# Odd layer's scan: the 128x128 transposes of each level become 64x64 products with the identity, and two products by tokens share one PSUM tile

## The chip, the cores and the metric

The kernel runs on one core of a Trainium2 chip. The metric is the device time of one execution in microseconds, the median of three runs.

## What is computed

The reference is a stack of two blocks of two layers each, on 512 tokens (and 256 context tokens) of width 1024. The change touches one part of the first block's odd layer: a recurrent scan with eight heads of 64 channels, run in two directions, first over the context and then over the tokens.

```python
def wkv7_scan(state0, p, d, reverse, emit):
    ...
    def step(S, inp):
        w_t, k_t, v_t, kk_t, a_t = inp[:5]
        sa = jnp.einsum('bhvk,bhk->bhv', S, kk_t)
        S = (S * w_t[:, :, None, :] - sa[..., None] * (kk_t * a_t)[:, :, None, :]
             + v_t[..., None] * k_t[:, :, None, :])
        return S, (jnp.einsum('bhvk,bhk->bhv', S, inp[5]) if emit else None)
```

The kernel computes this scan in chunks of 64 tokens. Within a chunk the 64 dependent steps become a triangular 64x64 system for each head, whose inverse X is built up in levels: blocks of 2, 4, ..., 32 rows are joined to blocks of twice the size.

## The kernel before, in words

The function `rwkv` holds the scan. Its work comes in **units**, `unit(d, i)`: one direction `d` (two) and one chunk `i` (twelve), 24 units in all, and in **blocks**, `block(d, g)`: the inputs of two chunks of one direction, 12 in all. Every unit and block is a generator; a loop over ticks starts a unit every third tick and a block nine ticks ahead of its first unit, and moves all that are alive by one step in each tick, so that six units or so are under way at once. What comes out of this is then ordered once more, for each engine, by the scheduler of the language, which weighs it by costs of its own; so a change in one step can move other instructions by a few places.

The eight heads lie as four groups of two: 64 partitions hold one head, the other 64 another. `prod` (line 1398) makes eight products of 64x64 tiles, one for each head. `pair` takes one of three PSUM tiles of two banks (pool `rwps`); the products of a head on the upper and on the lower partitions go to different banks. `seen` is the view by which a product is read back. In the profile these tiles are called `rw`.

One unit makes, in order: A (copied by ScalarE, line 1498) and X's first form (VectorE, lines 1502 and 1503); B (line 1509) and, for chunks of tokens, rb (line 1514), each with a PSUM tile of its own; a transposed copy kt of two inputs (lines 1521 and 1523); bv (line 1528); and then five levels. A level is

```python
for e in range(2):
    nc.tensor.transpose(ps[:, 0, P * e:P * e + P], X[:, 2 * e:2 * e + 2]..., ident)   # 1536
prod(ps, "J", "N", (grp(A), (lambda g: blk(X[:, g]))), base=256, step=32, n=32)
nc.scalar.copy(two(xt), ...)                                                          # 1539
nc.vector.tensor_tensor(out=two(w), ...)                                              # 1541
yield
prod(ps, "N", "J", (grp(xt), grp(w)), step=32, n=32)
nc.vector.tensor_tensor(out=xb, in0=xb, in1=s, op=ALU.subtract)                       # 1549
```

The transposes are two instructions on whole 128x128 tiles, all other products of the unit are on 64x64 tiles. After the levels come bv's correction, un (line 1561), the new state N (lines 1571 and 1572) and the output (lines 1583 to 1586, into the tile that the profile calls x).

A block makes, in this order: the low-rank products `ru` and `ra` (line 1447, TensorE, four instructions of 128x128 each), their tanh `th` (1448, ScalarE), `ld` (1458, GpSimd), the running sum `L` (1461, VectorE), `av` (1459) and `b` (1464) on GpSimd, exponentials on ScalarE (1468 to 1473), and on VectorE `kd`, `E` and the second `b` (1475 to 1481).

Of the kernel before, what the change touches and what calls it, by code (L numbers as in the profile page):

```python
# [12 lines left out]
ALU = mybir.AluOpType  # L13
# [3 lines left out]
P = 128  # L17
# [4 lines left out]
T = TX + TC  # L22
# [254 lines left out]
class Prog:  # L277
# [31 lines left out]
    c = v  # L309
# [1054 lines left out]
    def rwkv(self, R, mod, inner, parts, more):  # L1364
# [5 lines left out]
        nc, a = self.nc, self.a  # L1370
        DEC = float(np.exp(-0.5))
        with ExitStack() as es:
# [7 lines left out]
            i64 = self.c("i64")  # L1380
# [3 lines left out]
            pair = lambda: pps.tile([P, 1024], F32, tag="rw", name="rw").rearrange("p (b c) -> p b c", b=2)  # L1384
            of_c = lambda t_: t_.rearrange("p g c t -> p g (c t)")

            def prod(ps, lam, mu, *terms, base=0, step=64, at=0, n=64):

                lb, mb = LAY[lam][0], LAY[mu][0]
                bits = [0, 0, 0]  # L1390
                for bits[3 - lb - mb] in range(2):
                    for i, (L, Rb) in enumerate(terms):
                        for bits[lb] in range(2):
                            for bits[mb] in range(2):
                                g = 2 * bits[LAY[lam][1]] + bits[LAY[lam][2]]
                                h = HALF[bits[lb]]
                                o0 = base + step * bits[3 - lb - mb] + at
                                nc.tensor.matmul(ps[HALF[bits[mb]], bits[lb], o0:o0 + n], L(g)[h], Rb(g)[h],  # L1398
                                                 start=i == 0, stop=i == len(terms) - 1)

            def seen(ps, lam, mu, base=0, step=64, at=0, n=64):

                v = ps[:, :, base:base + 2 * step].rearrange("p b (s w) -> p b s w", s=2)[:, :, :, at:at + n]
                return v if LAY[mu][1] == LAY[lam][0] else v.rearrange("p b s w -> p s b w")

            grp = lambda t_: (lambda g: t_[:, g])
            two = lambda t_: t_.rearrange("p (x y) w -> p x y w", x=2)
            mask = lambda d, i, n=1: (mk[:, d, i:i + n].rearrange("p m q -> p (m q)").unsqueeze(1).unsqueeze(1)
                                      .to_broadcast([P, 2, 2, 64 * n]))
            ident = self.c("ident")  # L1410
# [73 lines left out]
            def unit(d, i):  # L1484
                ci = chunk(d, i)
                isx = ci >= 4
                E, b_, kd_, gc_, vt = blocks[d, ci // 2]
                c = ci % 2
                e0, e1 = (lambda g: E[:, g, c, 0]), (lambda g: E[:, g, c, 1])
                b, kd, v = (lambda g: b_[:, g, c]), (lambda g: kd_[:, g, c]), (lambda g: vt[:, c, g])  # L1490
                gc = gc_[:, :, c]
                nn = P if isx else 64
                ev = lambda g: E[:, g, c].rearrange("p e t -> p (e t)")[:, :nn]

                ps = pair()
                prod(ps, "N", "J", (e0, b))
                A = sm("A", 5)
                nc.scalar.copy(two(A), seen(ps, "N", "J"))
                ps = pair()
                prod(ps, "N", "J", (b, e0))  # L1500
                X = sm("X", 6)
                nc.vector.tensor_tensor(out=two(X), in0=seen(ps, "N", "J"), in1=mask(1 - d, 0), op=ALU.mult)
                nc.vector.tensor_tensor(out=X, in0=i64s, in1=X, op=ALU.subtract)
                yield

                ps = pair()
                prod(ps, "N", "T", (kd, ev), step=P, n=nn)
                B = sm("B", 6, nn)
                nc.vector.tensor_tensor(out=two(B), in0=seen(ps, "N", "T", step=P, n=nn), in1=mask(d, 6, nn // 64), op=ALU.mult)
                if isx:  # L1510
                    ps = pair()
                    prod(ps, "N", "T", (b, e1))
                    rb = sm("rb", 6)
                    nc.vector.tensor_tensor(out=two(rb), in0=seen(ps, "N", "T"), in1=mask(d, 7), op=ALU.mult)
                yield
                if i < 11:

                    ps = pair()
                    for q, t_ in enumerate((kd_, b_)):
                        for j in range(2):  # L1520
                            nc.tensor.transpose(ps[:, q, P * j:P * j + P], t_[:, 2 * j:2 * j + 2, c].rearrange("p e t -> p (e t)"), ident)
                    kt = up.tile([P, 2, 4, 64], F32, tag="kt", name="kt", bufs=5)
                    nc.scalar.copy(kt.rearrange("p q g f -> p q (g f)"), ps[:, :, 0:256])
                yield
                ps = pair()
                prod(ps, "T", "J", ((lambda g: B[:, g, 0:64]), v))
                bv = sm("bv", 5)
                nc.scalar.activation(out=two(bv), in_=seen(ps, "T", "J"), func=AF.Copy, scale=-1.0)
                yield

                for l in range(1, 6):

                    blk = lambda t_: t_.rearrange("p (n two b) -> p n two b", two=2, b=1 << l)[:, :, 1 - d]
                    ps = pair()
                    for e in range(2):
                        nc.tensor.transpose(ps[:, 0, P * e:P * e + P], X[:, 2 * e:2 * e + 2].rearrange("p h c -> p (h c)"), ident)  # L1536
                    prod(ps, "J", "N", (grp(A), (lambda g: blk(X[:, g]))), base=256, step=32, n=32)
                    xt, w = sm("xt", 3), sm("w", 3, 32)
                    nc.scalar.copy(two(xt), ps[:, 0, 0:256].rearrange("p (e j r) -> p j e r", e=2, j=2))
                    m = mk[:, d, l, 0:32].unsqueeze(1).unsqueeze(1).to_broadcast([P, 2, 2, 32])  # L1540
                    nc.vector.tensor_tensor(out=two(w), in0=seen(ps, "J", "N", base=256, step=32, n=32), in1=m, op=ALU.mult)
                    yield
                    ps = pair()
                    prod(ps, "N", "J", (grp(xt), grp(w)), step=32, n=32)
                    xb = X.rearrange("p (x y) (n two b) -> p x y n two b", x=2, two=2, b=1 << l)[:, :, :, :, 1 - d]
                    s = seen(ps, "N", "J", step=32, n=32).rearrange("p x y (n b) -> p x y n b", b=1 << l)
                    if l == 5:
                        xb, s = xb[:, :, :, 0], s[:, :, :, 0]
                    nc.vector.tensor_tensor(out=xb, in0=xb, in1=s, op=ALU.subtract)
                    yield  # L1550

                N = state[d]
                if N is not None:
                    ps = pair()
                    prod(ps, "N", "J", (e0, grp(N)))
                    nc.vector.tensor_tensor(out=two(bv), in0=two(bv), in1=seen(ps, "N", "J"), op=ALU.subtract)
                yield
                ps = pair()
                prod(ps, "J", "T", (grp(X), grp(bv)))
                un = sm("un", 3)  # L1560
                nc.scalar.copy(two(un), seen(ps, "J", "T"))
                yield
                if i < 11:
                    ps = pair()
                    prod(ps, "T", "N", ((lambda g: kt[:, 0, g]), v), ((lambda g: kt[:, 1, g]), grp(un)))
                    N2 = sm("N", 3)
                    gcb = gc.unsqueeze(2).to_broadcast([P, 4, 64])
                    if N is None:
                        nc.vector.tensor_tensor(out=two(N2), in0=seen(ps, "T", "N"), in1=two(gcb), op=ALU.mult)
                    else:  # L1570
                        nc.vector.tensor_tensor(out=two(N2), in0=two(N), in1=seen(ps, "T", "N"), op=ALU.add)
                        nc.vector.tensor_tensor(out=N2, in0=N2, in1=gcb, op=ALU.mult)
                    state[d] = N2
                yield
                if isx:

                    ps = pair()
                    prod(ps, "N", "J", (grp(N), e1))
                    prod(ps, "T", "J", (v, (lambda g: B[:, g, 64:P])), (grp(un), grp(rb)), base=P)
                    c4 = ci - 4  # L1580
                    yy = two(y[:, :, 64 * c4:64 * c4 + 64])
                    if (c4 < 4) == (d == 0):
                        nc.scalar.copy(yy, seen(ps, "N", "J"))
                    else:
                        nc.vector.tensor_tensor(out=yy, in0=yy, in1=seen(ps, "N", "J"), op=ALU.add)
                    nc.vector.tensor_tensor(out=yy, in0=yy, in1=seen(ps, "T", "J", base=P), op=ALU.add)
                done.add((d, i))
# [485 lines left out]
    def ssd_part(self, n, hi, lo, sp, R):  # L2073
# [22 lines left out]
        def prep(g, r):  # L2096
            def feature(nm, j):
                def done(ps):
                    r[nm] = tl(nm, [n], 1 if nm == "B" else 2)
                    self.ssd_conv(j, ps, n, sp, cbuf, r[nm])  # L2100
                    yield
                    if nm == "B":
                        for _ in range(6):
# [365 lines left out]
```

## Time and profile before

| what | value |
|---|---|
| runs | 4059.23, 4055.31, 4044.3 us; median 4055.31 us |
| profiled execution | 4060.4 us, of it the span 4058.7 us |
| mean granted TensorE clock of the span | 0.968 |
| busy in the span | TensorE 94%, weight loads 77%, VectorE 58%, ScalarE 38%, GpSimd 7% |
| the scan | from 1390 to 1710 us of the span |

In the rows further down, PE is TensorE, PEld its weight loads (which overlap PE), DVE VectorE, ACT ScalarE, POOL GpSimd. `rw<-X,A 64*64 64x32 f32` is a product into tile rw of the operands X and A on a 64x64 tile of the array. An f32 product shows as two instructions, so a `prod` of eight products reads x16; a transpose shows as one. Busy times of TensorE overlap and their ends are modelled, so what a group costs is read from its start to the next group's start.

### The profile page before, as it was taken

The numbers are of one execution on the slowest core, as the hardware profiler recorded it, in microseconds if no ns is written. First come the engines' busy times: TensorE is split into PE (matmuls) and PEld (weight loads), VectorE is DVE, ScalarE is ACT, GpSimd is POOL, SyncE is SP. The second block draws the span as 40 slices with busy tenths as digits, with TensorE's granted clock in tenths as the row PEclk, the third lists the DMA queues.
The fourth block names the chain that finished last, engine by engine and source line by source line (L and its number), as shares of the span: only waits on it lengthen the run. The fifth ranks groups of instructions, "written<-read, shape, count | busy, mean of one in ns | idle before, by whom it ended". The sixth has DMA issues, their size and how long they took to land.

```text
span 4058.7 us, 68289 instructions
## 1 busy us (share of the span) xinstructions
PE 3832.5 (94%) x28564; PEld 3110.9 (77%) x28564; DVE 2348.8 (58%) x4086; ACT 1554.3 (38%) x2862; POOL 294.7 (7%) x310
## 2 busy tenths in 40 slices
PE   7999999999999898899999999999998999989998
PEld 5667788888877676678877877888887777767887
DVE  6556555545645455577664466455458788784334
ACT  4456321212445344342233333212126576663222
POOL 0222000000010011000000000000001222120000
PEclk8999999999999979999999998999998999999999
DMA  4221133333214311145541102333333233322232
GB/s 176 85 84 41 63 110 116 115 107 100 75 50 140 117 42 40 31 147 177 165 146 60 65 30 72 116 116 116 102 96 122 82 108 109 120 73 83 94 95 87
DMA packets 144196, 393.08 MB, mean 97 GB/s; under 512 B 14096, under 2 KB 45712, under 8 KB 142992
## 3 DMA queue, kind: packets, MB, share of 16 engines
q1 hardware_dynamic: 143888, 388.72, 29.0%
q8 instruction: 224, 3.67, 0.4%
q14 instruction: 84, 0.69, 0.1%
HBM read 374.38 MB, written 14.29 MB: 96 GB/s over the span
## 4 chain that ended last, share of the span: by engine, by line
PE 80%; DVE 9%; issue 4%; ACT 4%; DMA 1%; POOL 1%; SPq 0%; DVEq 0%; ACTq 0%; POOLq 0%
PE mm L418 18%; PE mm L359 15%; PE mm L361 15%; PE mm L363 15%; PE mm L388 4%; PE rw L1398 2%; PE y L900 2%; PE tp L887 2%; PE y L2342 1%; PE rw L1536 1%; DVE cva L2068 1%; DVE wlo L340 1%; PE s L817 1%; ACT whi L339 1%; PE s L818 0%
## 5 line engine op out<-in xcount | busy, mean ns | idle before, releaser
L339 ACT CAST whi<-w 128x1024 fp32r<-128x1024 f32 (+2 forms) x429 | 439.1, 1025 | 1588.0 <-PE mm L361 1004.3
L340 DVE TENSOR_TENSOR wlo<-w,whi 128x1024 fp32r<-128x1024 f32 (+2 forms) x429 | 518.0, 1208 | 329.9 <-ACT whi L339 321.2
L359 PE MATMUL mm<-fhi,whi 128*128 128x512 f32 x2016 | 610.0, 356 | 0.0
L361 PE MATMUL mm<-flo,whi 128*128 128x512 f32 x2016 | 609.4, 356 | 0.0
L363 PE MATMUL mm<-fhi,wlo 128*128 128x512 f32 x2016 | 607.5, 355 | 0.0
L363 PEld LDWEIGHTS mm<-fhi,wlo 128*128 128x128 f32 x2016 | 331.3, 187 | 61.3
L359 PEld LDWEIGHTS mm<-fhi,whi 128*128 128x128 f32 x2016 | 331.4, 187 | 60.8
L361 PEld LDWEIGHTS mm<-flo,whi 128*128 128x128 f32 x2016 | 331.4, 187 | 59.4
L475 DVE SCALAR_TENSOR_TENSOR wdot<-wmod,cb 128x1024 f32<-128x1024 f32 x288 | 352.0, 1222 | 9.6 <-ACT cb L469 3.6
L626 DVE SCALAR_TENSOR_TENSOR x<-mm,mod,x 128x512 f32<-128x512 f32 (+1 forms) x214 | 131.9, 643 | 339.4 <-PE mm L363 270.2
L738 DVE TENSOR_TENSOR g<-g,mm 128x512 f32<-128x512 f32 (+1 forms) x134 | 75.6, 590 | 403.4 <-PE mm L363 395.7
L359 PE MATMUL mm<-ah,whi 128*128 128x512 f32 x972 | 294.0, 356 | 0.0
L361 PE MATMUL mm<-al,whi 128*128 128x512 f32 x972 | 293.8, 356 | 0.0
L363 PE MATMUL mm<-ah,wlo 128*128 128x512 f32 x972 | 293.0, 355 | 0.7 <-DVE wlo L340 0.7
L363 PEld LDWEIGHTS mm<-ah,wlo 128*128 128x128 f32 x972 | 159.7, 187 | 30.6 <-DVE wlo L340 1.1
L359 PEld LDWEIGHTS mm<-ah,whi 128*128 128x128 f32 x972 | 159.7, 187 | 29.4
L361 PEld LDWEIGHTS mm<-al,whi 128*128 128x128 f32 x972 | 159.7, 187 | 28.8
L838 POOL TENSOR_SCALAR p<-p,st 128x256 f32<-128x256 f32 (+3 forms) x128 | 95.7, 748 | 1008.9 <-DVE st L837 917.7
L418 PE MATMUL mm<-shi,whi 128*128 128x512 f32 x328 | 138.8, 423 | 0.0
L418 PE MATMUL mm<-shi,wlo 128*128 128x512 f32 x328 | 131.1, 401 | 2.9 <-DVE wlo L340 2.9
L418 PE MATMUL mm<-slo,whi 128*128 128x512 f32 x328 | 131.9, 402 | 0.0
L2068 DVE SCALAR_TENSOR_TENSOR cva<-cvb,v_ssd,cva 128x512 f32<-128x512 f32 (+1 forms) x176 | 121.7, 704 | 11.7 <-ACT cva L2066 9.6
(573 smaller groups left out, 7339.9 us busy)
## 6 DMA issues: line engine op xcount, KB each, us to landing
wmod<-wmod SPq DMA_DIRECT2D x176, 512.0 KB, 3.8
w<-wfi SPq DMA_DIRECT2D x176, 512.0 KB, 3.3
w<-ws_in SPq DMA_DIRECT2D x62, 512.0 KB, 3.3
w<-wfo SPq DMA_DIRECT2D x64, 448.0 KB, 3.4
w<-wfo SPq DMA_DIRECT2D x32, 512.0 KB, 3.5
rb<-acd SPq DMA_DIRECT2D x32, 512.0 KB, 3.9
w<-wo_in SPq DMA_DIRECT2D x26, 512.0 KB, 3.3
w<-wa_in SPq DMA_DIRECT2D x21, 512.0 KB, 3.3
```

The costliest lines, as they stand in the source:

```text
L339: self.nc.scalar.copy(hi, src)
L340: (engine or self.nc.vector).tensor_tensor(out=lo, in0=src, in1=hi.bitcast(F32), op=ALU.subtract)
L359: nc.tensor.matmul(o, whi(k), ah(k), start=s, stop=False)
L361: nc.tensor.matmul(o, whi(k), al(k), start=False, stop=False)
L363: nc.tensor.matmul(o, wlo(k), ah(k), start=False, stop=e)
L388: self.nc.tensor.matmul(o, w[:, k], x[:, k, t0:t0 + n], start=s, stop=e)
L418: self.nc.tensor.matmul(o, w[:, k], x[:, k, t0:t0 + n], start=s, stop=e)
L475: dot = nc.vector.scalar_tensor_tensor(out=t, in0=w, scalar=1.0, in1=cb[:, i], op0=ALU.mult, op1=ALU.mult, accum_out=out[:, j, i:i + 1])
L626: self.nc.vector.scalar_tensor_tensor(out=x, in0=ps, scalar=mod[:, i_g + m, i:i + 1], in1=x, op0=ALU.mult, op1=ALU.add)
L838: nc.gpsimd.tensor_scalar(out=p, in0=p, scalar1=l, scalar2=1.0, op0=ALU.mult, op1=ALU.mult)
L887: nc.tensor.transpose(ps[:, k * P:k * P + P], p[:, (k0 + k) * P:(k0 + k + 1) * P], self.c("ident"))
L2068: nc.vector.scalar_tensor_tensor(out=acc, in0=pc[:, t:t + n], scalar=w(t), in1=acc, op0=ALU.mult, op1=ALU.add)
```

## The change

Each level's two transposes become a `prod` of eight products with the 64x64 identity `i64`, into columns 0 to 127 of both banks; xt is read back by `seen`. And rb's products go into columns 256 to 383 of B's PSUM tile, behind B's products, so that a unit of tokens takes one PSUM tile less.

```diff
                 ps = pair()
                 prod(ps, "N", "T", (kd, ev), step=P, n=nn)
+                if isx:
+                    prod(ps, "N", "T", (b, e1), base=256)
                 B = sm("B", 6, nn)
                 nc.vector.tensor_tensor(out=two(B), in0=seen(ps, "N", "T", step=P, n=nn), in1=mask(d, 6, nn // 64), op=ALU.mult)
                 if isx:
-                    ps = pair()
-                    prod(ps, "N", "T", (b, e1))
                     rb = sm("rb", 6)
-                    nc.vector.tensor_tensor(out=two(rb), in0=seen(ps, "N", "T"), in1=mask(d, 7), op=ALU.mult)
+                    nc.vector.tensor_tensor(out=two(rb), in0=seen(ps, "N", "T", base=256), in1=mask(d, 7), op=ALU.mult)
...
                     ps = pair()
-                    for e in range(2):
-                        nc.tensor.transpose(ps[:, 0, P * e:P * e + P], X[:, 2 * e:2 * e + 2].rearrange("p h c -> p (h c)"), ident)
+                    prod(ps, "J", "N", (grp(X), (lambda g: i64)))
                     prod(ps, "J", "N", (grp(A), (lambda g: blk(X[:, g]))), base=256, step=32, n=32)
                     xt, w = sm("xt", 3), sm("w", 3, 32)
-                    nc.scalar.copy(two(xt), ps[:, 0, 0:256].rearrange("p (e j r) -> p j e r", e=2, j=2))
+                    nc.scalar.copy(two(xt), seen(ps, "J", "N"))
```

The order on the engines moves in two ways. On TensorE, in the tenth block's stretch (the products of X with the identity are those that read `consts` before and `c_odd` now; the numbers are those of the tiles), before:

```order
L1536 MATMUL rw_15578<-consts_60,X_14596 128x128 x2
L1398 MATMUL rw_15578<-X_14596,A_14585 64x32 x8
L1398 MATMUL rw_15593<-w_15538,xt_15537 64x32 x8
L1536 MATMUL rw_15603<-consts_60,X_15065 128x128 x2
L1398 MATMUL rw_15603<-X_15065,A_15054 64x32 x8
L1398 MATMUL rw_15620<-vt_14058,B_15459 64x64 x8
L1398 MATMUL rw_15646<-b_14563,E_14669 64x64 x8
L1398 MATMUL rw_15657<-E_14669,b_14563 64x64 x8
```

and now:

```order
L1398 MATMUL rw_15949<-c_odd_10997,X_14863 64x64 x8
L1398 MATMUL rw_15949<-X_14863,A_14852 64x32 x8
L1398 MATMUL rw_15970<-w_15909,xt_15908 64x32 x8
L1398 MATMUL rw_15980<-c_odd_10997,X_15390 64x64 x8
L1398 MATMUL rw_15980<-X_15390,A_15379 64x32 x8
L1398 MATMUL rw_16003<-vt_14267,B_15833 64x64 x8
L1398 MATMUL rw_16029<-b_14830,E_14948 64x64 x8
L1398 MATMUL rw_16040<-E_14948,b_14830 64x64 x8
```

The order of the groups is the same; two instructions on 128x128 became eight on 64x64 in each of the two levels, and every group now has the same tile size.

On VectorE in the same stretch (b is the block's instruction that reads GpSimd's b; w and X are the levels' masks and updates), before:

```order
L1549 TENSOR_TENSOR X_15065<-X_15065,rw_15541 128x64x2
L1541 TENSOR_TENSOR w_15538<-rw_15526,rmask_10994 128x128
L1549 TENSOR_TENSOR X_14836<-X_14836,rw_15593 128x16x8
L1541 TENSOR_TENSOR w_15590<-rw_15578,rmask_10994 128x128
L1477 TENSOR_TENSOR b_15633<-b_15633,em_15631 128x4x2x64
L1541 TENSOR_TENSOR w_15615<-rw_15603,rmask_10994 128x128
L1475 TENSOR_TENSOR kd_15634<-kd_15634,kk_15364 128x4x2x64
L1481 TENSOR_TENSOR kd_15634<-kd_15634,em_15631 128x4x2x64
L1502 TENSOR_TENSOR X_15666<-rw_15657,rmask_10994 128x256
```

and now:

```order
L1548 TENSOR_TENSOR X_15390<-X_15390,rw_15912 128x64x2
L1540 TENSOR_TENSOR w_15909<-rw_15891,rmask_10994 128x128
L1477 TENSOR_TENSOR b_16016<-b_16016,em_16014 128x4x2x64
L1540 TENSOR_TENSOR w_15967<-rw_15949,rmask_10994 128x128
L1548 TENSOR_TENSOR X_15132<-X_15132,rw_15970 128x16x8
L1475 TENSOR_TENSOR kd_16017<-kd_16017,kk_15718 128x4x2x64
L1540 TENSOR_TENSOR w_15998<-rw_15980,rmask_10994 128x128
L1481 TENSOR_TENSOR kd_16017<-kd_16017,em_16014 128x4x2x64
L1502 TENSOR_TENSOR X_16049<-rw_16040,rmask_10994 128x256
```

One X update and one w, which stood ahead of b, now stand behind it. This is so in five of the twelve blocks (the sixth, eighth and tenth to twelfth); in the seventh only the w moved. In the others the move is different or there is none.

## Rows read from the trace of the kernel before

**Rows 1.** Windows: us, busy PE, PEld, DVE, ACT, POOL (instructions), granted clock, DMA share, GB/s
```profile
1390.00:1710.00 320.00, 280.22 (x8413) 225.84 (x8414) 188.39 (x508) 136.05 (x348) 28.85 (x42) 0.92 0.16 44
...
1430.00:1452.00 22.00, 22.00 (x446) 17.81 (x444) 9.10 (x26) 8.11 (x20) 0.73 (x2) 0.50 0.14 39
1463.00:1470.00 7.00, 7.00 (x139) 5.74 (x140) 3.02 (x10) 1.34 (x3) 0.62 (x1) 0.52 0.13 38
1509.00:1521.00 12.00, 12.00 (x185) 10.03 (x184) 6.47 (x16) 3.69 (x8) 0.73 (x2) 0.50 0.17 47
```

**Rows 2.** The chain that ended last, 1390 to 1710 us, by line
```profile
by line: PE rw L1398 29.3%; issue 17.8%; PE rw L1536 10.6%; PE mm L1447 4.8%; POOL b L1464 4.1%; DVE L L1461 3.3%; PE mm L418 2.7%; DVE w L1541 2.6%; PE rw L1521 2.5%; ACT xt L1539 2.5%; POOL av L1459 1.9%; ACT th L1448 1.9%; POOL ld L1458 
```

**Rows 3.** Instructions by line and shape, 1390 to 1710 us: busy, mean ns | idle before
```profile
L1536 PE MATMUL rw<-consts,X 128*128 128x128 f32 x240 | 55.8, 317 | 15.6 <-DVE x L1586 10.7 <-DVE X L1502 3.4 <-ACT un L1561 0.7
L1539 ACT COPY xt<-rw 128x256 f32<-128x256 f32 x120 | 44.5, 371 | 124.9 <-PE rw L1398 124.9
L1398 PEld LDWEIGHTS rw<-X,A 64*64 64x64 f32 x1920 | 42.5, 143 | 24.7 <-issue 24.7
...
L1561 ACT COPY un<-rw 128x256 f32<-128x256 f32 x24 | 9.0, 375 | 1.8 <-PE rw L1398 1.5
```

**Rows 4.** Timeline of PE, tenth block, full clock: start, us [idle before <- releaser]
```profile
1569.58 0.41 PE L1398 MATMUL rw<-w,xt 64*64 64x32 f32 x16
1569.93 0.44 PE L1536 MATMUL rw<-consts,X 128*128 128x128 f32 x2
1570.30 0.43 PE L1398 MATMUL rw<-X,A 64*64 64x32 f32 x16
1570.55 0.44 PE L1398 MATMUL rw<-vt,B 64*64 64x64 f32 x16
1570.81 0.41 PE L1398 MATMUL rw<-b,E 64*64 64x64 f32 x16
1572.32 0.46 PE L1398 MATMUL rw<-E,b 64*64 64x64 f32 x16 [1.09 <-DVE w L1541]
...
1573.98 0.44 PE L1536 MATMUL rw<-consts,X 128*128 128x128 f32 x2 [0.53 <-DVE X L1502]
```

**Rows 5.** Timeline of PE where the granted clock is 0.50
```profile
1436.40 0.69 PE L1398 MATMUL rw<-vt,B 64*64 64x64 f32 x16
1436.86 0.65 PE L1398 MATMUL rw<-b,E 64*64 64x64 f32 x16
...
1438.49 0.69 PE L1536 MATMUL rw<-consts,X 128*128 128x128 f32 x2
1439.11 0.66 PE L1398 MATMUL rw<-X,A 64*64 64x32 f32 x16
```

**Rows 6.** Timeline of DVE, tenth block
```profile
1570.06 0.29 DVE L1549 TENSOR_TENSOR X<-X,rw 128x128 f32<-128x128 f32 x1 [2.12 <-PE rw L1398]
1570.27 0.28 DVE L1541 TENSOR_TENSOR w<-rw,rmask 128x128 f32<-128x128 f32 x1
1571.37 0.69 DVE L1477 TENSOR_TENSOR b<-b,em 128x512 f32<-128x512 f32 x1 [0.81 <-POOL b L1464]
1571.98 0.28 DVE L1541 TENSOR_TENSOR w<-rw,rmask 128x128 f32<-128x128 f32 x1
...
1573.50 0.42 DVE L1502 TENSOR_TENSOR X<-rw,rmask 128x256 f32<-128x256 f32 x1
```

**Rows 7.** Timeline of POOL, tenth block
```profile
1570.06 1.28 POOL L1464 TENSOR_TENSOR b<-kx,av 128x512 f32<-128x512 f32 x1
```

**Rows 8.** The page: instructions of TensorE, and the DMA queue of instructions
```profile
PE 3832.5 (94%) x28564; PEld 3110.9 (77%) x28564; DVE 2348.8 (58%) x4086; ACT 1554.3 (38%) x2862; POOL 294.7 (7%) x310
...
q8 instruction: 224, 3.67, 0.4%
```

**Rows 9.** Waits, 1390 to 1710 us (us in total, times, longest); timeline of PE
```profile
PE rw L1398 <- issue: 4.1, 10, 1.0
...
1586.96 0.37 PE L1398 MATMUL rw<-X,A 64*64 64x32 f32 x11 [0.96 <-issue]
```

## The prediction

> **What bounds the kernel now.** I went from the table of stretches to the chain of waits, then to the groups by line, and last to the timeline of a few places. The scan is the only stretch that the change touches: 320 of 4058.7 us, in which TensorE is busy 280 us and VectorE 188 us [rows 1]. So TensorE is close to being the bound here, with 40 us of gaps. The chain of waits says how close: of the 320 us, 29.3% are the 64x64 products, 10.6% the transposes of line 1536, and smaller shares go through GpSimd's b, VectorE's L and w, and ScalarE's copies [rows 2]. It runs over TensorE for a while, crosses to a block's preparation on ScalarE, GpSimd and VectorE, and comes back. What TensorE saves counts where the chain is on TensorE, and is lost where the block's preparation sets the pace.
>
> Two things in the groups by line are to be seen. The weight loads of the product X,A, which always follow a level's transposes, sat idle 24.7 us "for nothing that the profile shows" [rows 3]: 120 levels, 0.2 us each, at the change from 128x128 to 64x64 tiles. And ScalarE's copy xt waited for line 1398, not for line 1536 [rows 3]: it starts only when the products behind the transposes in the same PSUM tile are done, and will do so after the change too.
>
> **The transposes.** From start to start, at full clock: transposes 0.37 us (1569.93 to 1570.30), X,A to the next 64x64 group 0.25 us, a 64x64 group of 16 to the next one 0.26 us (1570.55 to 1570.81), and the group ahead of a transpose 0.35 us (1569.58 to 1569.93) where it would take 0.25 us ahead of another 64x64 group [rows 4]. So a level's transposes cost 0.37 + 0.10 = 0.47 us of TensorE, and eight products with the identity, the same shape as vt,B, should cost 0.26 us: 0.21 us less. Where TensorE was waiting before the transposes (as at 1573.98, [rows 4]) the 0.10 us was hidden in the wait, and only 0.11 us is saved. At half clock the transposes take 0.62 us (1438.49 to 1439.11) and a 64x64 group 0.46 us (1436.40 to 1436.86) [rows 5]: 0.16 us less, and again about 0.10 us ahead of it.
>
> How many count? The half-clock stretches hold 446 + 139 + 185 = 770 of the scan's 8413 product instructions [rows 1], at 70 a level 11 of the 120 levels, so a transpose pair takes (109 x 0.37 + 11 x 0.62) / 120 = 0.39 us on average. The chain has 10.6% of 320 = 34 us of them [rows 2], so 34 / 0.39 = 87 of the 120 levels lie on it. Of these 76 at full clock save 0.11 us and 11 at half clock 0.16 us: 10 us. The other 0.10 us is saved where TensorE came to the transposes without a wait; 15.6 us of idle time stand before line 1536 [rows 3], in waits of 0.5 us or more like that at 1573.98, so in about 25 cases; some 60 of the 87 are left, 6 us. **Term: -16 us.** Bounds: all 120 levels at the whole price, 109 x 0.21 + 11 x 0.26 = -26 us; and 0 if what comes after always waits for a block.
>
> [...]
>
> **VectorE's order.** b (line 1477) waits for GpSimd's b, which runs 1.28 us [rows 7]; VectorE sat 0.81 us before it [rows 6]. Everything behind b on VectorE waits too. Before, that was one w (1571.98), which held up E,b on TensorE for 1.09 us [rows 4]. Now, in five blocks, one more X update (0.29 us) and one more w (0.28 us) stand behind b. TensorE's next groups, vt,B and b,E, need PSUM tiles that these two set free: before they ran at 1570.55, right behind that w (1570.27 + 0.28) [rows 4, 6]. Now vt,B can start only after b and w, at about 1571.37 + 0.69 + 0.28 = 1572.3. That alone costs nothing, because TensorE would stand still until 1572.32 in any case; but what VectorE does between b and X of line 1502 grows by 0.29 + 0.28 = 0.57 us, and the transposes at 1573.98 wait for that X [rows 4, 6]. Five and a half blocks x 0.57 us: **+3 us.** Bounds: nothing if GpSimd's b comes earlier by as much, because TensorE reaches the block's `ra` sooner; at the worst vt,B's whole shift, 1572.3 - 1570.55 = 1.75 us, in all twelve blocks, +21 us. I take the sum of the two moved instructions, since vt,B's shift falls into time in which TensorE now waits.
>
> **More instructions.** TensorE's 28564 products and as many weight loads came through the instruction queue as 224 packets of 3.67 MB [rows 8]: 64 bytes each, 256 to a packet. A level had 2 and gets 16 of each kind, 120 x 28 = 3360 more, 13 packets. Ten times in the scan TensorE stops, most often in the middle of a group, for nothing shown: 4.1 us, as 0.96 us at 1586.96 [rows 9]; I take it that instructions were late. In 66 packets' worth of instructions (16827 in the scan, [rows 1]) that makes 0.06 us a packet: **+1 us**; bounds 0 and 13 x 0.96 = +12 us.
>
> **The shared PSUM tile, and the copy.** B's mask now waits for rb's eight products too, 0.26 us by the same row, in 16 units; in return 16 PSUM tiles fewer are taken from a pool of three. Each side is worth at most 16 x 0.26 = 4 us; I take **0**. The copy xt reads two banks now; un, which already does, takes 375 ns against 371 ns [rows 3]: 120 x 4 ns, **0**.
>
> **Sum:** -16 + 3 + 1 = -12 us. The profiled execution (4060.4 us, its span and 1.7 us around it) would come to 4048 us; the median shown is 5 us below it, so the forecast for the median is 4055.3 - 12 = **4043 us**.
>
> **Rivals.**
> *TensorE alone sets the pace* (chance 0.17). All 120 levels pay in full, and the scheduler's new order hides the blocks: -26 us, 4029 us. For it: TensorE is busy 280 of 320 us. Against: 40 us of gaps, most of them behind VectorE and the blocks.
> *b holds VectorE, and through it TensorE* (0.12), the case on the other side. If GpSimd's b does not come earlier and vt,B's shift is paid in every block, 12 x 1.75 = +21 us, the late instructions add 3 us more, and the levels give back 16: 4055 + 8 = 4063 us. It decides as soon as the shift costs more than 16 / 12 = 1.3 us a block. For it: the wait is in the trace now, and vt,B has a new one. Against: TensorE stands still there already.
> *The granted clock changes* (0.18). [...] Without them the 41 us would be 41 x 0.26 / 0.46 = 23: -18 us more, 4025 us (0.10). With as many again, +18: 4061 us (0.08).
> *The small products do not pack* (0.03). [...]
>
> **Chances and range.** The forecast has 0.50. Three runs lie within 15 us, 0.37%, so about 0.5% (20 us) is what a measurement of this kernel can tell from no change: faster means below 4035, slower above 4075.6. Below 4035 lie the first rival, the clock's better half, and a tail of the forecast whose unknown terms all fall on the good side, but not always beyond the line: 0.14 + 0.09 + 0.04 = 0.27. Above 4075.6 lies only b's case together with a worse clock: 0.04. The rest, 0.69, is within. The range reaches to 4017 (the first rival with part of the clock's gain) and 4066 (b's case with 3 us over).
>
> **What would show it.** Right: line 1536 is gone and a group rw<-c_odd,X of 16 takes about 0.26 us to the next start at full clock; the idle time before X,A's weight loads falls from 24.7 us to a few; the groups ahead of the identity's products take 0.25 us in place of 0.35. The scan is some 12 us shorter, and nothing else moves. Wrong: vt,B waits for w of VectorE for over 1.3 us in most blocks, or stops inside groups become many, or the half-clock stretches are of another length than 41 us.

## The result: slower, and the profile after

The changed kernel takes 4077.5 us (median of six runs, 4072.5 to 4085.6) against 4048.0 us for the kernel before on the same chip (six runs, 4038.2 to 4059.2): a ratio of 1.0075, interval 1.0063 to 1.0088. It is slower by 30 us; the forecast was 12 us faster, and the time lies outside its range. The profiled execution of the changed kernel took 4078.5 us (span 4076.7), close to its median; that of before lies 12 us above its own, so the two spans differ by 18 us only. The mean granted clock of that execution of before was low for this kernel, 0.968; in 49 other runs of it, beside the experiments below, it was 0.970 to 0.976.

TensorE's line and the instruction queue, on the page of the changed kernel:

```profile
PE 3817.5 (94%) x30244; PEld 3119.3 (77%) x30244; DVE 2349.3 (58%) x4086; ACT 1554.9 (38%) x2862; POOL 293.8 (7%) x310
...
q8 instruction: 237, 3.88, 0.4%
```

1680 products, 1680 weight loads and 13 packets of instructions more than in [rows 8], as counted. The scan's last product now starts at 1726.3 us instead of 1708.2. Its stretch in the table of stretches of the changed kernel (columns as in [rows 1]):

```profile
1390.00:1726.00 336.00, 264.22 (x10065) 233.18 (x10063) 185.37 (x502) 136.83 (x348) 28.55 (x41) 0.91 0.14 40
```

Against the first line of [rows 1], TensorE's busy time fell by 16.0 us (280.2 to 264.2), at nearly the same granted clock (0.92 and 0.91), and its idle time rose by 32 us (39.8 to 71.8). So TensorE got less to do and did it later. What it waited for, in the table of waits of the changed kernel, 1390 to 1750 us (us in total, times, longest):

```profile
PEld rw L1398 <- issue: 43.0, 51, 1.8
PE rw L1398 <- issue: 32.9, 36, 1.7
...
PEld rw L1398 <- DVE w L1540: 23.8, 27, 2.2
DVE b L1477 <- POOL b L1464: 20.1, 11, 3.5
PE rw L1398 <- DVE w L1540: 19.3, 24, 2.1
```

The second line is the answer to [rows 9]: stops for nothing that the profile shows were 4.1 us in 10 places, and are 32.9 us in 36. The last two are the second thing that grew: VectorE waits longer for GpSimd's b, and TensorE for the w behind it. Before, they read (1390 to 1710 us):

```profile
PE rw L1398 <- DVE w L1541: 10.3, 25, 1.1
...
DVE b L1477 <- POOL b L1464: 8.4, 10, 1.2
```

The groups by line and shape of the changed kernel, 1390 to 1750 us:

```profile
L1398 PE MATMUL rw<-c_odd,X 64*64 64x64 f32 x1920 | 63.0, 246 | 14.6 <-DVE x L1585 5.8 <-issue 5.1 <-DVE w L1540 1.3
L1538 ACT COPY xt<-rw 128x256 f32<-128x256 f32 x120 | 44.5, 371 | 131.8 <-PE rw L1398 131.1
...
L1398 PEld LDWEIGHTS rw<-X,A 64*64 64x64 f32 x1920 | 48.1, 151 | 8.9 <-issue 8.9
...
L1398 PE MATMUL rw<-vt,B 64*64 64x64 f32 x384 | 12.4, 240 | 12.2 <-DVE w L1540 10.9 <-issue 1.3
```

The weight loads of X,A stand idle 8.9 us instead of 24.7 [rows 3], so the change of tile size inside a level is gone. (The transposes of kt, line 1521, are on 128x128 tiles too, in both kernels; they were left out above, where all other products of a unit were said to be on 64x64 tiles.) The copy xt costs 371 ns as before. vt,B waits 12.2 us, 10.9 of them for w. The timeline of PE around the tenth block shows this wait, and the price of a group:

```profile
1573.15 0.41 PE L1398 MATMUL rw<-c_odd,X 64*64 64x64 f32 x16
1573.39 0.39 PE L1398 MATMUL rw<-X,A 64*64 64x32 f32 x16
1573.59 0.41 PE L1398 MATMUL rw<-w,xt 64*64 64x32 f32 x16
1573.89 0.46 PE L1398 MATMUL rw<-c_odd,X 64*64 64x64 f32 x16
1574.17 0.39 PE L1398 MATMUL rw<-X,A 64*64 64x32 f32 x16
1576.61 0.46 PE L1398 MATMUL rw<-vt,B 64*64 64x64 f32 x16 [2.04 <-DVE w L1540]
```

A group with the identity takes 0.24 us to the next start (1573.15 to 1573.39) or 0.28 (1573.89 to 1574.17); 0.26 was forecast. X,A takes 0.20 us to the next group (1573.39 to 1573.59), where 0.25 stood in [rows 4]. vt,B's wait has the form foreseen: on DVE, b waited 3.4 us for GpSimd's b, and the w ran behind it:

```profile
1575.66 0.69 DVE L1477 TENSOR_TENSOR b<-b,em 128x512 f32<-128x512 f32 x1 [3.39 <-POOL b L1464]
1576.27 0.28 DVE L1540 TENSOR_TENSOR w<-rw,rmask 128x128 f32<-128x128 f32 x1
```

Now the stops. In the timeline of PE from 1643 to 1663 us they come at an even beat, in the middle of groups of all kinds:

```profile
1647.61 0.28 PE L1398 MATMUL rw<-c_odd,X 64*64 64x64 f32 x3 [1.19 <-issue]
1651.32 0.25 PE L1398 MATMUL rw<-w,xt 64*64 64x32 f32 x3 [0.87 <-issue]
1655.35 0.38 PE L1398 MATMUL rw<-c_odd,X 64*64 64x64 f32 x9 [1.14 <-issue]
1658.92 0.39 PE L1398 MATMUL rw<-c_odd,X 64*64 64x64 f32 x10 [0.79 <-issue]
1662.40 0.21 PE L1398 MATMUL rw<-B,vt 64*64 64x64 f32 x1 [1.03 <-issue]
```

The table of stretches from stop to stop counts what lies between:

```profile
1647.61:1651.32 3.71, 2.56 (x128) 2.33 (x127) 2.01 (x5) 0.74 (x2) 0.00 (x0) 1.00 0.02 4
1651.32:1655.35 4.03, 2.88 (x129) 2.54 (x129) 1.30 (x5) 1.61 (x4) 0.00 (x0) 1.00 0.01 4
1655.35:1658.92 3.57, 2.43 (x128) 2.15 (x128) 1.86 (x6) 0.92 (x3) 0.00 (x0) 1.00 0.02 5
1658.92:1662.40 3.48, 2.45 (x129) 2.29 (x129) 1.97 (x6) 0.74 (x2) 0.00 (x0) 1.00 0.02 5
```

That is 128 products and 128 loads each time (a record more or less): one packet of 256 instructions. TensorE has 2.4 to 2.9 us of work in them and gets the next packet after 3.5 to 4.0 us.

### The profile page after: what moved, and what is told of

It reads as the page before. It is cut to its first block, busy times and chain, and to the rows that moved or that the text cites. A ratio compares the mean times of both kernels' runs of the same rounds, so it can differ in the third digit from the quotient of the medians.

```text
span 4076.7 us, 71666 instructions
## 1 busy us (share of the span) xinstructions
PE 3817.5 (94%) x30244; PEld 3119.3 (77%) x30244; DVE 2349.3 (58%) x4086; ACT 1554.9 (38%) x2862; POOL 293.8 (7%) x310
## 4 chain that ended last, share of the span: by engine, by line
PE 81%; DVE 8%; ACT 4%; issue 4%; DMA 2%; POOL 1%; SPq 0%; DVEq 0%; ACTq 0%; POOLq 0%
PE mm L418 17%; PE mm L359 14%; PE mm L361 14%; PE mm L363 14%; PE mm L388 4%; PE rw L1398 3%; PE y L900 2%; PE tp L887 2%; PE y L2341 1%; DVE cva L2067 1%; DVE wlo L340 1%; PE s L817 1%; ACT whi L339 1%; PE s L818 0%; DMA wm<-wmod 0%
```

## The theories

**A, supply.** TensorE's instructions arrive at one packet of 256 per 3.5 to 4 us at the best (as read above). Where its work in a packet is shorter (2.4 to 2.9 us in the stretches above), TensorE stops. **B, the shared PSUM tile.** B's mask comes later, and the work behind it. **C, VectorE's order.** b holds up w and, through it, vt,B. Beside them the granted clock.

## The experiments

All ratios are against runs of the kernel before on the same chip.

**Only the identity products, and only the shared tile.** The diff of the change, split in two: the first has the hunk at lines 1532 to 1541 alone, the second the hunk at lines 1505 to 1514 alone.

> The identity products alone; rb keeps its own PSUM tile. Theory A (instructions come in packets of 256, one per 3.4 to 4.0 us, and TensorE runs out of them): the 13 packets more are all here, so all of the loss is here, +25 to +32 us against before; waits of TensorE for nothing shown in the scan about 33 us, as in the changed kernel. Theory B (the shared PSUM tile makes B's mask late): no loss, -12 us as forecast. Theory C (VectorE's new order around b): VectorE's order is that of the changed kernel, so also +25 to +32 us, but in waits of vt,B for w, and with few stops for nothing shown.

> rb in B's PSUM tile, the transposes as before. Theory A: no instruction more or less, VectorE's order around b as before: within 4 us of before. Theory B: +25 us or more.

Identity products alone: 4081.5 us, ratio 1.0075 (1.0060 to 1.0091). Shared tile alone: 4045.7 us, 0.9990 (0.9979 to 1.0001). The stops, in the table of waits of the first and then of the second:

```profile
PE rw L1398 <- issue: 37.2, 44, 1.6
```

```profile
PE rw L1398 <- issue: 3.0, 8, 0.7
```

The whole loss comes with the identity products, and the stops with it. B falls: the shared tile costs nothing that shows, as forecast.

**Fewer, wider instructions.** The transposed copies by four products on 64x128 tiles (16 instructions a level, loads among them, in place of 32), or by four transposes on the same tiles (8 a level). Each is set in place of the line with `i64` in the changed kernel:

```diff
-                    prod(ps, "J", "N", (grp(X), (lambda g: i64)))
+                    for hf in range(2):
+                        for e in range(2):
+                            nc.tensor.matmul(ps[:, hf, 64 * e:64 * e + 64], X[HALF[hf], 2 * e:2 * e + 2].rearrange("p h c -> p (h c)"),
+                                             i64[HALF[hf]], start=True, stop=True)
```

(the second with `nc.tensor.transpose` and the same operands).

> The changed kernel, but the identity products are 4 on tiles of 64 rows and 128 columns in place of 8 on 64x64: 16 instructions a level in place of 32 (before: 4). VectorE's order around b is that of the changed kernel. Theory A: 1440 instructions more than before in place of 3360, 5.6 packets in place of 13; the loss falls to less than half, 0 to +12 us, and the stops for nothing shown with it, to 10 to 18 us. Theory C: the loss stays at +25 to +32 us, vt,B waits for w as long as in the changed kernel (11 us in all).

> The changed kernel, but the identity products are 4 transposes on tiles of 64 rows and 128 columns: 8 instructions a level (before 4, changed 32). Theory A: 480 instructions more than before, 2 packets: stops for nothing shown near those of before, 4 to 8 us, and the time at or below before, -10 to +2 us. Theory C: +25 us or more, since VectorE's order around b is that of the changed kernel.

Four products: 4106.9 us, 1.0131 (1.0108 to 1.0154), far above what either theory gave. The stops did go (PE 3.6 us in 8 places), but the instructions are slow; timeline of PE of this run:

```profile
1561.93 0.41 PE L1398 MATMUL rw<-w,xt 64*64 64x32 f32 x16
1562.28 0.67 PE L1537 MATMUL rw<-c_odd,X 64*128 64x64 f32 x8
1562.87 0.43 PE L1398 MATMUL rw<-X,A 64*64 64x32 f32 x16
```

A group of eight takes 0.59 us (1562.28 to 1562.87), against 0.24 or 0.28 us for sixteen on 64x64 tiles, and the change of tile size is back: the group ahead takes 0.35 us (1561.93 to 1562.28), as it did ahead of the transposes [rows 4]. The mean granted clock was low too, 0.961 over six runs. So this run does not test the supply. Four transposes: 4062.7 us, 1.0023 (1.0010 to 1.0036), 12 runs. Stops 7.5 us, clock 0.966:

```profile
PE rw L1398 <- DVE w L1542: 12.0, 20, 1.4
...
PE rw L1398 <- issue: 7.5, 11, 2.3
```

A quarter of the level's instructions, and a quarter of the stops: in the stops A holds. In the time it does not: some 9 us slower than before by the ratio, where -10 to +2 were expected (more on this under the dose). vt,B does not wait in this run (0.0 us): VectorE's order came out nearly as before, against the expectation, so the run does not tell A from C.

**b behind the masks.** The changed kernel with b issued one step later and ordered behind the last but one w, so that the w no longer stands behind GpSimd's b:

```diff
+                bm = lambda: nc.vector.tensor_tensor(out=b, in0=b, in1=em, op=ALU.mult)
...
+                    with self.tc.issue_after(masks[-2]):
+                        bm()
...
```

> The changed kernel with VectorE's order set by hand: each block's b stands behind the two masks w and the X updates that the changed kernel has behind it. Instructions as in the changed kernel. Theory A (supply of instructions alone): stays at +20 to +32 us against before, stops for nothing shown about 33 us. Theory C (VectorE's order around b): vt,B's waits for w (11 us) go, and 11 us or more of the loss with them: +5 to +18 us.

4073.9 us, 1.0064 (1.0052 to 1.0077). vt,B's group and the stops:

```profile
L1398 PE MATMUL rw<-vt,B 64*64 64x64 f32 x384 | 12.0, 233 | 2.7 <-DVE w L1546 2.3 <-issue 0.2
```

```profile
PE rw L1398 <- issue: 34.5, 40, 1.7
```

vt,B's wait fell from 12.2 to 2.7 us, and the stops stayed. Of the loss some 4 us went, by the two ratios (1.0075 and 1.0064), whose intervals overlap. So C's wait is real, but its price is small and not clear of noise.

**The identity products in bf16.** They read the upper halves of X and a copy of the identity in bf16 (`i64h`), so xt is X cut to bf16, a change of the computation: one instruction and one load for each product in place of two, 16 a level in place of 32.

```diff
...
-                    prod(ps, "J", "N", (grp(X), (lambda g: i64)))
+                    half = lambda t_: t_.bitcast(mybir.dt.bfloat16)
+                    prod(ps, "J", "N", ((lambda g: half(X)[:, g, 1::2]), (lambda g: i64h)))
```

> The changed kernel, but the identity products read the upper halves of X and of the identity as bf16 (X^T then has only bf16's digits): one instruction for each product and each load in place of two, so 16 instructions a level in place of 32 (before 4), same tile size, same places. Theory A: 1920 instructions fewer than the changed kernel, 7.5 packets of 13; the stops for nothing shown fall from 33 to about 10 to 18 us, and the time by 12 us or more, to +15 us or less against before. Theory C: VectorE's order around b is about that of the changed kernel, so the loss stays above +20 us.

4055.9 us, 1.0017 (1.0008 to 1.0026), 11 runs. The loss goes from 30 to 8 us, the stops from 32.9 to 24.0:

```profile
PE rw L1398 <- issue: 20.3, 25, 1.5
...
L1398 PE MATMUL rw<-i64h,X 64*64 64x64 bf16 x960 | 33.5, 208 | 16.0 <-DVE x L1588 5.7 <-issue 3.7 <-ACT un L1563 3.0
```

The time is as A expected, the stops are not (10 to 18 us). And the run is no clean test: the bf16 group is also much shorter, 0.07 us to the next start, where 0.26 us was the price in f32. That alone takes some 20 us of TensorE's work out of 120 levels (an estimate from these lines):

```profile
1587.58 0.26 PE L1398 MATMUL rw<-i64h,X 64*64 64x64 bf16 x8
1587.65 0.42 PE L1398 MATMUL rw<-X,A 64*64 64x32 f32 x16
```

Stops remain: the scan's work is now 258.3 us in 71 packets, 3.6 us a packet, which is still within the 3.5 to 4.0 us from packet to packet. VectorE's order came out nearly as in the kernel before here too (vt,B waits 1.7 us), so C is not tested. These runs have a low mean clock, 0.966.

**The supply by itself.** The kernel before, with constant products behind the scan that nothing needs: 640 of 64 columns and then 256 of 256 columns on 64x64 tiles (each leaves two records and two loads).

```diff
...
+            for n, many in ((64, 160), (256, 64)):
+                ps = pair()
+                for _ in range(many):
+                    for k in range(4):
+                        lb, mb = k // 2, k % 2
+                        nc.tensor.matmul(ps[HALF[mb], lb, 0:n], i64[HALF[lb]], ones[HALF[lb], 0:n], start=True, stop=True)
...
```

> The kernel before with products added behind the scan, on 64x64 tiles, of constants alone: 640 with 64 columns (561 of them in one piece) and 256 with 256 columns, nobody waits for them. Theory A: in the first piece TensorE stops every 128 product instructions (256 with the loads), and the stretch from stop to stop is 3.4 to 4.0 us though 128 of them need only 2.1 us; in the second, where 128 need over 4 us, there is no stop. Without a limit of supply there are no stops in either.

One execution, 4109.8 us. Timeline of PE, in the added products (the first line is at a granted clock of 0.50, the others at 1.00):

```profile
1720.72 6.68 PE L1644 MATMUL rw<-c_odd 64*64 64x64 f32 x256 [3.62 <-issue]
1727.94 2.09 PE L1644 MATMUL rw<-c_odd 64*64 64x64 f32 x128 [0.54 <-issue]
1731.41 2.09 PE L1644 MATMUL rw<-c_odd 64*64 64x64 f32 x128 [1.38 <-issue]
1734.88 2.09 PE L1644 MATMUL rw<-c_odd 64*64 64x64 f32 x128 [1.38 <-issue]
1738.35 2.09 PE L1644 MATMUL rw<-c_odd 64*64 64x64 f32 x128 [1.38 <-issue]
1742.37 2.09 PE L1644 MATMUL rw<-c_odd 64*64 64x64 f32 x128 [1.93 <-issue]
1746.39 28.32 PE L1644 MATMUL rw<-c_odd 64*64 64x64 f32 x541 [1.93 <-issue]
```

These products have no operand to wait for. Every 128 products (a packet, with their loads) TensorE works 2.09 us and stops: a packet per 3.47 us (1731.41 to 1734.88), at times per 4.02 us. The last line holds the wide products, 28.32 us without one stop, some 7 us for 128 of them. At half the clock (first line, behind a longer stop) 256 products, two packets, run 6.68 us without a stop inside. So A is shown without the scan: at full clock TensorE stopped where a packet's work lasted 2.09 us, and did not where it lasted some 7. That the work must last about 3.5 to 4 us is an estimate from the beat of 3.47 and 4.02 us.

The packets themselves are in the trace, in the DMA queue of instructions, and nothing else moves in these stretches. One packet comes in between two stops: it starts 1.1 to 1.7 us after TensorE has gone on (1.06 in the stretch from 1731.41), takes 0.9 to 1.0 us, and TensorE goes on some 1.4 us after it has landed. So most of the 3.47 us is not the transfer itself. It is the same in the five stretches of the changed kernel's scan from 1643.86 to 1662.40 us: each has one packet, of 16384 bytes, and nothing else in its DMA queues; it starts 1.1 to 1.6 us after TensorE has gone on, takes 0.9 to 1.2 us, and TensorE goes on 1.2 to 1.6 us after it has landed. In the scans of the kernel before and of the changed kernel no packet starts less than 3.29 and 3.31 us after the one ahead. With the added products of 64 columns TensorE stood still for 1.38 us, at times 1.93, behind each 2.09 us of work.

**The dose.** Identity products in the first level of each unit alone (24 of 120), and in the first three (72); the shared tile in both. The first:

```diff
...
+                    if l <= 1:
+                        prod(ps, "J", "N", (grp(X), (lambda g: i64)))
+                    else:
+                        for e in range(2):
+                            nc.tensor.transpose(ps[:, 0, P * e:P * e + P], X[:, 2 * e:2 * e + 2]..., ident)
...
```

> The changed kernel with the identity products in the first level of each unit alone (24 of 120 levels); the other 96 levels keep their two transposes; rb shares B's PSUM tile. 24 x 28 = 672 more instructions on TensorE, 2.6 packets. Theory A (each packet of 256 instructions is paid where TensorE works densely): the loss grows with the number of levels. With the shared tile alone the time was 4045.7 us, with all 120 levels 4077.5: 32 us over 120 levels, so 24 levels cost 6 us, about 4052 us, and the stops named issue come to about 3 + 24/120 x 30 = 9 us. Rival (a threshold: the supply matters only once the whole scan needs more packets than its time can bring, and below it the levels give back their 0.21 us): 4041 to 4046 us, stops as in the kernel before.

> As the run with 24 levels, with the identity products in the first three levels of each unit (72 of 120). 72 x 28 = 2016 more instructions, 7.9 packets. Theory A, a loss in proportion: 32 x 72/120 = 19 us, about 4065 us, stops about 3 + 18 = 21 us. Rival (a threshold): less than half of the loss of the full change, 4045 to 4060 us.

24 levels: 4060.2 us, 1.0035 (1.0021 to 1.0048). 72 levels: 4065.8 us, 1.0048 (1.0035 to 1.0061). The stops, of 24 and then of 72 levels:

```profile
PE rw L1398 <- issue: 8.3, 13, 1.3
```

```profile
PE rw L1398 <- issue: 18.2, 24, 1.4
```

The stops are near those that A gave, 9 and 21 us. The rival with a threshold falls: the stops rise with the first 24 levels already (3.0 to 8.3 us), and both times lie above what it gave. The time at 72 levels is as expected, though some 7 us of it go with the granted clock (below), and at 24 the loss against the shared tile alone is 14 us where 6 were expected. Most of that goes with the clock, too. In the 49 runs of the kernel before, on three chips, the mean clock of a run lies between 0.970 and 0.976 and goes with its time: 2.3 us longer per 0.001 lower (correlation -0.77). The mean clock was 0.9734 with the shared tile alone, 0.9692 with 24 levels, 0.9703 with 72 and with 120. Brought to the clock of before (0.9731) by that slope, continued a little below the range that it was read from, the mean times are 4047.5, 4052.3, 4060.6 and 4071.4 us: 4.8, 13.1 and 23.9 us for 24, 72 and 120 levels, 0.20, 0.18 and 0.20 us a level. Each of these is good to some 5 us, as the intervals of the ratios are. An estimate from rows gives nearly this for A: 28 more instructions a level take 28/256 of a packet's 3.47 us, 0.38 us, and spare TensorE 0.21 us: 0.17 us lost a level.

By the same slope, taken further down, the four transposes would come to 4045 us and the bf16 products to 4038 us, against a mean of 4049.5 us before. So the clock may be what hides a small gain in both; this is a reckoning, and no run shows it.

## Why the prediction was wrong

**The step that failed is "More instructions", +1 us with bounds 0 and +12.** The 13 packets were right. The price was the ten stops of before spread over its 66 packets, 0.06 us each, as if a packet cost the same however fast it is used up. At that pace it cost next to nothing: 280.2 us of work in 66 packets is 4.3 us a packet on average [rows 1], more than the 3.5 to 4.0 us that the next one takes. But the average hides how near the edge that was: in the scan of the kernel before, 32 of the 65 packets start less than 4.0 us after the one ahead, and in that of the changed kernel 48 of 78. The change takes work out and puts instructions in: 264.2 us in 79 packets, 3.4 us a packet, less than the 3.5 to 4.0 us from one packet to the next. So nearly every packet in a dense piece may stop TensorE, not the 13 new ones alone; the bound of 13 x 0.96 us was wrong for the same reason. The stops grew by 32.9 - 4.1 = 28.8 us.

**The transposes, -16 us:** right in the price of a group (0.24 and 0.28 us about the forecast 0.26), and X,A's loads lost 15.8 us of idle time. That TensorE's busy time fell by just 16.0 us is luck: the 16 us of the forecast are those on the chain, and by its own price all 120 levels were to free TensorE of 26 us. Most of the saving did not reach the end, because TensorE then stopped for instructions (32.9 us).

**VectorE's order, +3 us:** right in kind. vt,B waits for w 1.5 to 2.1 us in six of the twelve blocks, 10.9 us in all, about the 1.75 us that the prediction set as the worst for a block. In return E,b's wait for w fell from 7.9 to 3.6 us, so part of the shift did fall into time in which TensorE waited already; TensorE's waits for w grew by 9.0 us together (10.3 to 19.3). The run with b moved prices the shift at some 4 us, not clear of noise. It is the rival *b holds VectorE*, with its mechanism there and its price too small to decide.

**The shared tile and the copy, 0:** right within the noise, by the run with the shared tile alone (0.9979 to 1.0001) and by xt's 371 ns.

**The granted clock**, a rival with a chance of 0.18 (its 41 us are the three stretches at 0.50 to 0.52 in [rows 1]), seems to be part of it: the mean clock of the changed kernel's runs was 0.9703 against 0.9731, by the slope above 2.8 x 2.3 = 6 us of the 30. Between the two profiled executions it is not what differs: their scans have 0.91 and 0.92, and still end 18 us apart. What lowers the mean clock is open: it was lower in every kernel with the transposed copies in another form (means of 0.961 to 0.971) and not in the two without (0.973), and no experiment here changed the clock by itself.

**The rivals** *TensorE alone sets the pace* and *The small products do not pack* fell: TensorE was idle 72 us, and no run shows small products that do not pack; a group of sixteen took 0.24 or 0.28 us, about the 0.26 us of [rows 4]. "Stops inside groups become many" stood among the signs of a wrong forecast, but had no case and no chance of its own.

**Together:** 24 us at equal clock against the shared tile alone and 6 us that go with the clock, less 2 us that the shared tile gives back, are 28 us; the mean time differs by as much from that of the 49 runs, the medians of the result by 30. The parts are taken from these same times, so the sum is a split of the loss and no check of it. Of the 24, the stops are 29, vt,B's wait is up to 4, and about 9 us of TensorE's saving is what reached the end. This split, too, is a sum that must close, not something a run shows by itself.

## What to carry to other kernels

Count TensorE's instructions, loads too, as a resource of their own: divide its busy time by its packets of 256, and do it for the dense pieces, as the average over a stretch is too kind. With 24 levels the scan had 4.1 us of work a packet and 8.3 us of stops, with the shared tile alone 4.0 us a packet and 3.0 us of stops; their granted clocks in the scan were 0.90 and 0.98, and a low clock lengthens the average (a group of sixteen takes 0.46 us at 0.50 and 0.26 us at 1.00, [rows 4, 5]). Where a packet held 2.1 to 2.9 us of work here, it came every 3.5 to 4 us; in such a piece a further instruction costs about 14 ns, an estimate from the added products (3.47 us / 256). So two large transposes a level, 0.37 us to the next start [rows 4], were better here than eight small products, 0.24 or 0.28 us: by 30 us in the result. The few short stops of the kernel before, ten with 4.1 us [rows 9], came where 32 of 65 packets were less than 4.0 us apart already; price such stops by the pace, not by their mean.

## What was not expected of the hardware

The even beat of the stops: 3.47 or 4.02 us a packet in the added products, 3.5 to 4.0 us in the scan; and that in the added products only 0.9 to 1.0 us of it is the packet's transfer. That a product on a 64x128 tile was so much slower than on a 64x64 one: eight records in 0.59 us against sixteen in 0.24 or 0.28 us. And that the mean clock was as low with 24 levels of 120 as with all of them (0.9692 and 0.9703); what lowers it stays open.
